# A decoder trunk on one core: scores of the undilated group with zero-padded queries, and the probabilities transposed one unit later

## Chip, core and metric

One core of a Trainium2 chip runs the whole kernel in one launch. The metric is the device time of one execution in microseconds. The kernel before took 806.12 us (median of 3 runs, 805.39 to 806.36).

## What is computed

Two layers on 256 tokens of width 1024, everything in float32. The first layer's mixer is dilated attention: three groups of 16 heads of 64, dilations 1, 4 and 16, each a causal band, whose outputs are mixed by a softmax over their log-denominators. The second layer's mixer is forgetting attention. After each mixer comes a SwiGLU block. The change is in the first group (dilation 1) of the first mixer:

```python
proj = (h @ w_in).reshape(B, S, N_GROUPS, 3, N_HEADS, HEAD_DIM)
for g, (window, dil) in enumerate(DILATED_PATTERNS):      # (128,1), (512,4), (2048,16)
    q = partial_rotary(proj[:, :, g, 0], pos)
    k = partial_rotary(proj[:, :, g, 1], pos)
    o, lse = dilated_band_attention(q, k, proj[:, :, g, 2], dil, window // dil)
...
s = einsum('bcnihd,bcnjhd->bcnhij', qb, kb) * D ** -0.5   # masked to the band
p = exp(s - m); den = p.sum(-1); o = (p / den) @ vb; lse = m + log(den)
```

## The kernel before

Precision is made by splitting: `split` turns a float32 value x into a high part (ScalarE copies it to the matmul type fp32r, L71) and a low part (VectorE takes x minus the high part, L72). `mm3` multiplies two split operands by three matmuls: high by high (L167), high by low (L168), low by high (L169). Every weight tile passes through this: SyncE loads `raw` (L86), ScalarE writes `wh`, VectorE writes `wl`. There are 5 `raw` buffers and 4 each of `wh` and `wl`.

The first mixer is a loop over 36 *units* (`a_units`), 9 for each *quad* of four heads (hq = 0 to 3): q and k of group 0, q and k of group 1, q and k of group 2, and the values of the three groups (quad 0 begins with the values of groups 1 and 2 and has the values of group 0 last). A unit is one projection: 48 matmuls of 256 columns into the PSUM tile `ps_mm`. Two heads share the 128 partitions, head h in rows 64h to 64h+63; two such pairs (`pr`) make a quad. After a q or k unit, `rotated` applies the rotary embedding: VectorE shuffles (L345) and multiplies by the cosine (L346), the sine is multiplied on VectorE for group 0 and on GpSimd for the others (L347), and VectorE adds (L348). For group 0 the result is split into one tile, `qkr`.

Work on the attention is put off by `later`, a table from unit to functions that are run after that unit's projection:

- `scores_a(quad, 0)` one unit after k of group 0: for each pair and each of two query blocks and two heads one `mm3`, 24 matmuls in all, into `ps_sc` (two buffers). A head's matmul contracts its 64 rows; k is the moving operand, read with every second element (`early`), since the tokens are kept in a permuted order. Then `softmax`: mask and scale (L238), maximum (L241) on VectorE, exponentials with sums on ScalarE (L232).
- `scores_a` for the groups 1 and 2 (L375, 16 matmuls of 64 columns for each group), and after group 2 `group_weights`, which scales the probabilities `p` (L248, four tiles on VectorE, two on GpSimd).
- `trans_a(quad, pr)` for each pair, after unit 9 hq + 10 + pr: three times four transposes (L254) into `ps_tr` (two buffers), each copied to `pt` by VectorE (L258). So the third group of four waits until the first copy has freed its buffer.
- `pv_a(quad, pr)`, after unit 9 hq + 11 + pr: probabilities by values (L265) into `ps_o`, whose result is split into `ot`.

The units 9 hq + 9 and following belong to the next quad, so the transposes of a quad stand among the projections of the next one; those of quad 3 run in `out_proj`. The framework's scheduler orders the instructions of each engine by priority; `first()` raises it. The tiles with tag `h` have four buffers: the two `xp` rows of the input at the start, `qkr`, and the rows `x` that the residual needs in `out_proj` (L495), loaded at units 24 and 28 (L452).

Of the kernel before, what the change touches and what calls it, by code (L numbers as in the profile page):

```python
# [10 lines left out]
F32 = mybir.dt.float32  # L11
F32R = mybir.dt.float32r
# [4 lines left out]
P = 128  # L17
D = 1024
S = 256
# [12 lines left out]
def trunk(ctx: ExitStack, tc: tile.TileContext, T, out):  # L32
    nc = tc.nc
# [3 lines left out]
    ap = ctx.enter_context(tc.tile_pool(name="ap", bufs=1))  # L37
    ps = ctx.enter_context(tc.tile_pool(name="ps", bufs=1, space=bass.MemoryType.PSUM))

    ALL = slice(None)  # L40

    def first():

        return tc.high_priority(offset=300)

    def psum(tag):
        return ps.tile([P, 512], F32, tag=tag, name=f"ps_{tag}", bufs=2)

    def hrow(name):
        return ap.tile([P, D], F32, tag="h", name=name, bufs=4)  # L50
# [7 lines left out]
    def const(name, shape):  # L58
        c = cst.tile(shape, F32, name=name)
        nc.sync.dma_start(c, T[name])  # L60
        return c
# [6 lines left out]
    def split(pair, view, src, early=True):  # L68
        hi, lo = pair
        with first() if early else nullcontext():  # L70
            nc.scalar.activation(view(hi), src, AF.Copy)  # L71
            nc.vector.tensor_tensor(view(lo), src, view(hi).bitcast(F32), op=ALU.subtract)  # L72
# [52 lines left out]
    def weights(nm, i):  # L125
        upto = order.index((nm, i)) + AHEAD
        while state["next"] <= min(upto, len(order) - 1):
            key = order[state["next"]]
            ready[key] = piece(key)
            state["next"] += 1  # L130
        return ready.pop((nm, i))
# [33 lines left out]
    def mm3(o, stat, mov, start, stop):  # L165
        (sh, sl), (mh, ml) = stat, mov
        nc.tensor.matmul(o, sh, mh, start=start, stop=False)  # L167
        nc.tensor.matmul(o, sh, ml, start=False, stop=False)  # L168
        return nc.tensor.matmul(o, sl, mh, start=False, stop=stop)  # L169

    def both(pair, *idx):
        return tuple(x[idx] for x in pair)


    def early(x, b):

        x = x.rearrange("p (n b) -> p b n", b=2)
        return x if b is None else x[:, b]
# [23 lines left out]
    def p_tile():  # L202
        return ap.tile([P, 512], F32, tag="p", name="p", bufs=8)
# [27 lines left out]
    def exps(s, nm, den, j):  # L231
        nc.scalar.activation(s, s, AF.Exp, bias=nm[:, j:j + 1], accum_out=den[:, j:j + 1])  # L232

    def softmax(sc, mask, nm, den, i, g):

        s = p_tile()
        f = lambda x: x.rearrange("p (a b) -> p a b", b=mask.shape[-1])
        nc.vector.scalar_tensor_tensor(f(s), f(sc), HD ** -0.5, mask, op0=ALU.mult, op1=ALU.add)  # L238
        m = nm.rearrange("p (i g) -> p i g", g=NG)[:, i, g]
        sv = s.rearrange("p (i g j) -> p i g j", i=m.shape[1], g=m.shape[2])  # L240
        nc.vector.tensor_reduce(m, sv, axis=AX.X, op=ALU.max, negate=True)  # L241
        for x in range(m.shape[1]):
            for y in range(m.shape[2]):
                exps(sv[:, x, y, :], nm, den, (i.start + x) * NG + g.start + y)
        return sv
# [21 lines left out]
    def stat_tile(tag, n):  # L267
        return ap.tile([P, n], F32, tag=tag, name=tag, bufs=3)
# [66 lines left out]
    x = []  # L335
# [3 lines left out]
    def rotated(o, tag, eng):  # L339

        q = ap.tile([P, 2, S], F32, tag=tag, name=tag, bufs=2)
        tmp = ap.tile([P, 2, S], F32, tag="qr", name="rt", bufs=3)
        ov = o.rearrange("p (a b) -> p a b", a=2)
        with first():
            nc.vector.stream_shuffle(tmp, ov, [i ^ 8 if i < ROT else i for i in range(32)])  # L345
            nc.vector.tensor_tensor(q, ov, rcos[:, None, :].to_broadcast([P, 2, S]), op=ALU.mult)  # L346
        eng.tensor_tensor(tmp, tmp, rsin[:, None, :].to_broadcast([P, 2, S]), op=ALU.mult)  # L347
        nc.vector.tensor_tensor(q, q, tmp, op=ALU.add)  # L348
        return q

    def scores_a(quad, g):

        q, k = quad["fm"][g, 0], quad["fm"][g, 1]
        nm, den, pt = quad["nm"], quad["den"], quad["pt"]
        hr = (slice(0, 64), slice(64, 128))
        if g == 0:
            for pr in range(2):
                sc = [psum("sc") for _ in range(2)]
                for qb in range(2):
                    for h in range(2):  # L360
                        mm3(sc[h][:, qb * S:(qb + 1) * S], both(q, hr[h], pr, slice(qb * P, (qb + 1) * P)),
                            [early(x[hr[h], pr, :], None) for x in k], True, True)
                for h in range(2):
                    pt[pr, h] = softmax(sc[h], mask0, nm, den, slice(h * 4 + pr * 2, h * 4 + pr * 2 + 2), slice(0, 1))
            return

        if g == 1:
            quad["sc"] = [psum("sc") for _ in range(2)]
        sc = quad["sc"]
        for b in range(4):  # L370
            for h in range(2):
                for a in range(2):
                    c = slice(b % 2 * P + a * 64, b % 2 * P + a * 64 + 64)
                    o = b * P + (g - 1) * 64
                    nc.tensor.matmul(sc[h][a * 64:a * 64 + 64, o:o + 64], q[hr[h], b // 2, c], k[hr[h], b // 2, c],  # L375
                                     start=True, stop=True)
        if g == 2:
            m = mask12[:, None, :].to_broadcast([P, 4, P])
            for h in range(2):
                pt[h] = softmax(sc[h], m, nm, den, slice(h * 4, h * 4 + 4), slice(1, NG))  # L380
# [54 lines left out]
    def later(i, fn, *a):  # L435
        due.setdefault(i, []).append((fn, a))

    quad = None
    for i, (hq, g, w) in enumerate(a_units):
        if i % 9 == 0:  # L440
            quad = {"hq": hq, "fm": {}, "pt": {}, "v": {}, "nm": stat_tile("nm", 24), "den": stat_tile("den", 24)}
        wt, o = lead[i] if i < 2 else (weights("a_in", hq * 9 + g * 3 + w), psum("mm"))
        if i == 1:
            rcos = const("rcos", [P, S])
            rsin = const("rsin", [P, S])
        if i == 2:
            mask0 = const("mask0", [P, 2, S])
            mask12 = const("mask12", [P, P])
        if i in (24, 28):
            x.append(hrow("x"))  # L450
            t = len(x) - 1
            nc.sync.dma_start(x[t], T["x"][t * P:(t + 1) * P, :])  # L452
        if w < 2:
            for c in range(2):
                proj_feat(xt, wt, o[:, c * S:(c + 1) * S], c)
            if i == 2:
                rb = psum("tr")
                for t in range(2):
                    nc.tensor.matmul(rb[:, t * P:(t + 1) * P], r_a[t].to_broadcast([P, P]), ident,
                                     start=True, stop=True)  # L460
                for c in (rcos, rsin):
                    nc.vector.tensor_tensor(c, c, rb[:, :S], op=ALU.mult)
                rt = ap.tile([P, 2], F32, tag="rt", name="rt", bufs=1)
                tmp = ap.tile([P, D], F32, tag="xn", name="rd", bufs=2)[:, :S].rearrange("p (b c) -> p b c", b=2)
                e = early(rb[:, :S], None)
                nc.vector.tensor_tensor(tmp, e, ident[:, None, :].to_broadcast([P, 2, P]), op=ALU.mult)
                nc.vector.tensor_reduce(rt, tmp, axis=AX.X, op=ALU.add)
            q = rotated(o, f"fm{w}", nc.vector if g == 0 else nc.gpsimd)
            if g == 0:
                y = ap.tile([P, 2, 2, S], F32R, tag="h", name="qkr", bufs=4)  # L470
                f, q = q, (y[:, 0], y[:, 1])
                split(q, lambda y: y, f)
            quad["fm"][g, w] = q
            if w == 1:
                later(i + 1, scores_a, quad, g)
                if g == 2:
                    later(i + 1, group_weights, quad)
                    for pr in range(2):
                        later(9 * hq + 10 + pr, trans_a, quad, pr)
                        later(9 * hq + 11 + pr, pv_a, quad, pr)  # L480
        else:
            for t in range(i < 2, 2):
                proj_tok(xt, wt, o[:, t * S:(t + 1) * S], t, g == 0)
            values_a(quad["v"], g, o)
        for fn, a in due.pop(i, ()):
            fn(*a)
# [253 lines left out]
    for i, (hq, w) in enumerate(b_units):  # L740
# [4 lines left out]
        if w < 2:  # L745
            for c in range(2):
                proj_feat(xt, wt, o[:, c * S:(c + 1) * S], c)
            q = ap.tile([P, 2, S], F32, tag=f"fm{w}", name=f"fm{w}", bufs=2)
# [8 lines left out]
        else:  # L757
            for t in range(2):
                proj_tok(xt, wt, o[:, t * S:(t + 1) * S], t)
            q = v_tile(o)  # L760
# [32 lines left out]
    r = rstd(parts)  # L793
# [73 lines left out]
```

## Time and profile before

| | us |
|---|---|
| median of 3 runs | 806.12 |
| the profiled execution | 805.15 |
| its span in the trace | 803.4 |
| TensorE busy | 787.4 |
| VectorE busy | 555.4 |
| ScalarE busy | 421.2 |
| GpSimd busy | 59.9 |

The profiled execution is 0.97 us below the median, and its time lies 1.75 us above the span. In the lists below a row has a start, a length, the engine (PE is TensorE, PEld its weight loads, DVE VectorE, ACT ScalarE, POOL GpSimd, SP SyncE), the line, the tiles out<-in, the form (for a matmul rows*columns of the weights, then partitions x elements) and the count; in brackets stands idle time of the engine ahead of it and what ended that. Matmuls overlap: a row's length runs to the modelled end of the result, so what a matmul costs the engine is read from the distance between starts. The dilated mixer's units run from about 10 to 264 us, its output projection to about 294 us.

### The profile page before, as it was taken

What the parts mean: (1) busy time and instruction counts of PE and PEld (TensorE: products, weight loads), DVE (VectorE), ACT (ScalarE), POOL (GpSimd) and SP (SyncE); (2) the same over time, 40 slices, a digit from 0 to 9 for tenths busy, and PEclk for the clock granted to TensorE, in tenths of its full rate; (3) what the DMA queues carried; (4) which work ended last, traced back from release to release, by engine and by line L of the source; (5) the groups of instructions that cost most, each with busy time, mean ns of one, the idle gap of its engine ahead of it and who ended that gap; (6) DMA issues with size and microseconds to landing.
All of it is one profiled execution on the core that took longest, in us unless ns stands there. A gap on an engine that the chain in (4) does not pass through costs nothing.

```text
span 803.4 us, 13954 instructions
## 1 busy us (share of the span) xinstructions
PE 787.4 (98%) x5564; PEld 702.4 (87%) x5564; DVE 555.4 (69%) x829; ACT 421.2 (52%) x819; POOL 59.9 (7%) x76
## 2 busy tenths in 40 slices
PE   8999999999999999999999999999999999999996
PEld 7989899899999789888888879988879888888885
DVE  6798997986986685555657555677766756556643
ACT  7756347447445365455556545364535655546532
POOL 0010111011010110000000001211111000000001
PEclk9999999999999999999999999999999999999999
DMA  8856253734634346655556434543316665655601
GB/s 293 271 158 217 79 184 109 251 106 141 211 130 159 105 162 211 208 180 189 179 205 230 165 133 146 184 171 130 95 40 236 212 207 171 198 179 205 218 1 52
DMA packets 38833, 135.00 MB, mean 168 GB/s; under 512 B 4592, under 2 KB 5360, under 8 KB 38768
## 3 DMA queue, kind: packets, MB, share of 16 engines
q1 hardware_dynamic: 38624, 133.85, 49.9%
q8 instruction: 43, 0.70, 0.3%
q10 hardware_dynamic: 144, 0.26, 0.1%
q14 instruction: 22, 0.18, 0.1%
HBM read 133.05 MB, written 1.05 MB: 167 GB/s over the span
## 4 chain that ended last, share of the span: by engine, by line
PE 82%; DVE 10%; ACT 3%; issue 3%; DMA 1%; SPq 0%; POOL 0%; POOLq 0%; DVEq 0%
PE ps_mm L167 10%; PE ps_mm L169 10%; PE ps_mm L168 10%; PE ps_tr L198 9%; PE ps_mm L198 9%; PE ps_tr L199 4%; PE ps_mm L199 4%; PE ps_sc L167 4%; PE ps_sc L168 4%; PE ps_sc L169 4%; DVE wl L72 4%; PE ps_o L167 3%; PE ps_o L168 3%; PE ps_o L169 3%; ACT wh L71 2%
## 5 line engine op out<-in xcount | busy, mean ns | idle before, releaser
L72 DVE TENSOR_TENSOR wl<-raw,wh 128x1024 fp32r<-128x1024 f32 (+1 forms) x242 | 299.7, 1256 | 133.9 <-ACT wh L71 133.7
L71 ACT ACTIVATE wh<-raw 128x1024 fp32r<-128x1024 f32 (+1 forms) x242 | 248.3, 1048 | 165.2 <-issue 51.6
L167 PE MATMUL ps_mm<-xt,wh 128*128 128x256 f32 x512 | 147.4, 288 | 0.0
L168 PE MATMUL ps_mm<-xt,wh 128*128 128x256 f32 x512 | 145.4, 284 | 0.0
L169 PE MATMUL ps_mm<-xt,wl 128*128 128x256 f32 x512 | 145.4, 284 | 0.0
L198 PE MATMUL ps_tr<-xt,wh 128*128 128x512 f32 x304 | 109.6, 400 | 0.0
L198 PE MATMUL ps_mm<-xt,wh 128*128 128x512 f32 x304 | 108.1, 396 | 0.0
L167 PEld LDWEIGHTS ps_mm<-xt,wh 128*128 128x128 f32 x512 | 97.9, 191 | 3.1 <-issue 2.3
L168 PEld LDWEIGHTS ps_mm<-xt,wh 128*128 128x128 f32 x512 | 98.0, 191 | 1.5 <-issue 1.5
L169 PEld LDWEIGHTS ps_mm<-xt,wl 128*128 128x128 f32 x512 | 97.9, 191 | 1.0 <-issue 1.0
L167 PE MATMUL ps_mm<-wh,xt 128*128 128x256 f32 x304 | 86.6, 285 | 0.8 <-ACT wh L71 0.8
L168 PE MATMUL ps_mm<-wl,xt 128*128 128x256 f32 x304 | 86.0, 284 | 0.3 <-DVE wl L72 0.3
L169 PE MATMUL ps_mm<-wh,xt 128*128 128x256 f32 x304 | 85.8, 283 | 0.0
L199 PE MATMUL ps_tr<-xt,wl 128*128 128x256 f32 x304 | 85.1, 280 | 0.0
L199 PE MATMUL ps_mm<-xt,wl 128*128 128x256 f32 x304 | 84.9, 279 | 0.0
L198 PEld LDWEIGHTS ps_tr<-xt,wh 128*128 128x128 f32 x304 | 57.1, 188 | 15.1 <-DVE low L557 1.5
L198 PEld LDWEIGHTS ps_mm<-xt,wh 128*128 128x128 f32 x304 | 57.1, 188 | 13.2
L232 ACT ACTIVATE p<-p,nm 128x64 f32<-128x64 f32 (+2 forms) x128 | 51.4, 407 | 29.3 <-DVE nm L241 17.9
L167 PEld LDWEIGHTS ps_mm<-wh,xt 128*128 128x128 f32 x304 | 58.5, 192 | 1.7 <-ACT wh L71 1.4
L168 PEld LDWEIGHTS ps_mm<-wl,xt 128*128 128x128 f32 x304 | 58.4, 192 | 0.7 <-DVE wl L72 0.5
L169 PEld LDWEIGHTS ps_mm<-wh,xt 128*128 128x128 f32 x304 | 58.4, 192 | 0.0
L199 PEld LDWEIGHTS ps_mm<-xt,wl 128*128 128x128 f32 x304 | 57.2, 188 | 0.5
(213 smaller groups left out, 1271.5 us busy)
## 6 DMA issues: line engine op xcount, KB each, us to landing
raw<-in_gu SPq DMA_DIRECT2D x88, 512.0 KB, 4.3
raw<-in_a_in SPq DMA_DIRECT2D x70, 512.0 KB, 4.6
raw<-in_dn SPq DMA_DIRECT2D x44, 512.0 KB, 4.0
raw<-in_b_in SPq DMA_DIRECT2D x24, 512.0 KB, 4.6
raw<-in_a_out SPq DMA_DIRECT2D x8, 512.0 KB, 3.6
raw<-in_b_out SPq DMA_DIRECT2D x8, 512.0 KB, 3.5
grow<-in_norms SPq DMA_DIRECT2D x4, 512.0 KB, 5.6
xp<-in_x_perm SPq DMA_DIRECT2D x4, 256.0 KB, 4.6
```

What stands on the lines that cost most here:

```text
L71: nc.scalar.activation(view(hi), src, AF.Copy)
L72: nc.vector.tensor_tensor(view(lo), src, view(hi).bitcast(F32), op=ALU.subtract)
L167: nc.tensor.matmul(o, sh, mh, start=start, stop=False)
L168: nc.tensor.matmul(o, sh, ml, start=False, stop=False)
L169: return nc.tensor.matmul(o, sl, mh, start=False, stop=stop)
L198: nc.tensor.matmul(o.rearrange("p (x s) -> p x s", x=2), wh, xt.full[:, k], start=k == 0, stop=False)
L199: nc.tensor.matmul(o[:, :S], wl, xt[0][:, k], start=False, stop=k == KT - 1)
L232: nc.scalar.activation(s, s, AF.Exp, bias=nm[:, j:j + 1], accum_out=den[:, j:j + 1])
```

## The change

It has two parts, and a row of the input is loaded later.

1. Group 0's q is split into two tiles `qzh` and `qzl` of 2 x 2 x 256 elements a partition: plane h holds head h's rows, and zeros in the other head's 64 rows. GpSimd writes the zeros (four memsets of 64 x 512 a quad, L472), ScalarE and VectorE split each half by itself (two instructions of 64 x 512 each instead of one of 128 x 512). k is split into `kr` with its tokens already reordered, so that a read of 256 columns is contiguous. A score matmul now contracts all 128 rows, the other head's being multiplied by zero, and each head has its own `ps_sc` tile right before its softmax. There are still 24 matmuls a quad. Three buffers of tag `h` are taken in each quad instead of two.
2. `trans_a` and `pv_a` are put off to the units 9 hq + 11 + pr and 9 hq + 12 + pr.
3. The second row `x` is loaded at unit 31 instead of 28.

```diff
         if g == 0:
             for pr in range(2):
-                sc = [psum("sc") for _ in range(2)]
-                for qb in range(2):
-                    for h in range(2):
-                        mm3(sc[h][:, qb * S:(qb + 1) * S], both(q, hr[h], pr, slice(qb * P, (qb + 1) * P)),
-                            [early(x[hr[h], pr, :], None) for x in k], True, True)
                 for h in range(2):
-                    pt[pr, h] = softmax(sc[h], mask0, nm, den, slice(h * 4 + pr * 2, h * 4 + pr * 2 + 2), slice(0, 1))
+                    sc = psum("sc")
+                    for qb in range(2):
+                        mm3(sc[:, qb * S:(qb + 1) * S], both(q, ALL, h, pr, slice(qb * P, (qb + 1) * P)),
+                            both(k, ALL, pr, ALL), True, True)
+                    pt[pr, h] = softmax(sc, mask0, nm, den, slice(h * 4 + pr * 2, h * 4 + pr * 2 + 2), slice(0, 1))
             return
...
-        if i in (24, 28):
+        if i in (24, 31):
...
+            if g == 0 and w == 0:
+                qz = tuple(ap.tile([P, 2, 2, S], F32R, tag="h", name=f"qz{y}", bufs=4) for y in "hl")
+                for y in qz:
+                    for h in range(2):
+                        nc.gpsimd.memset(y[64 - h * 64:128 - h * 64, h].bitcast(F32), 0.0)
             q = rotated(o, f"fm{w}", nc.vector if g == 0 else nc.gpsimd)
-            if g == 0:
-                y = ap.tile([P, 2, 2, S], F32R, tag="h", name="qkr", bufs=4)
+            if g == 0 and w == 0:
+                for h in range(2):
+                    r = slice(h * 64, h * 64 + 64)
+                    split(qz, lambda y: y[r, h], q[r])
+                q = qz
+            elif g == 0:
+                y = ap.tile([P, 2, 2, S], F32R, tag="h", name="kr", bufs=4)
                 f, q = q, (y[:, 0], y[:, 1])
-                split(q, lambda y: y, f)
+                split(q, lambda y: y.rearrange("p a (b n) -> p a b n", b=2), f.rearrange("p a (n b) -> p a b n", b=2))
...
-                        later(9 * hq + 10 + pr, trans_a, quad, pr)
-                        later(9 * hq + 11 + pr, pv_a, quad, pr)
+                        later(9 * hq + 11 + pr, trans_a, quad, pr)
+                        later(9 * hq + 12 + pr, pv_a, quad, pr)
```

What this does to the order is shown at three places; the tiles have their numbers, so that buffers can be told apart. First TensorE at the first score matmuls of quad 2. Before, they follow the transposes of the second pair of quad 1 (`p_1210` and `p_1215`), and the two heads' tiles `ps_sc` take turns:

```order
L254 MATMUL ps_tr_1933<-ident_78,p_1210 128x128 x2
L254 MATMUL ps_tr_1933<-ident_78,p_1215 128x128 x2
L254 MATMUL ps_tr_1940<-ident_78,p_1210 128x128 x2
L254 MATMUL ps_tr_1940<-ident_78,p_1215 128x128 x2
L167 MATMUL ps_sc_1954<-qkr_1829,qkr_1761 128x256
L168 MATMUL ps_sc_1954<-qkr_1829,qkr_1761 128x256
L169 MATMUL ps_sc_1954<-qkr_1829,qkr_1761 128x256
L167 MATMUL ps_sc_1955<-qkr_1829,qkr_1761 128x256
L168 MATMUL ps_sc_1955<-qkr_1829,qkr_1761 128x256
L169 MATMUL ps_sc_1955<-qkr_1829,qkr_1761 128x256
```

Now the same place, where the transposes ahead are those of the first pair (the row shown is the last of four, `p_1169`), and one head's tile is filled after the other:

```order
L254 MATMUL ps_tr_1925<-ident_78,p_1169 128x128 x2
L167 MATMUL ps_sc_1939<-kr_1850,qzh_1769 128x256
L168 MATMUL ps_sc_1939<-kr_1850,qzh_1769 128x256
L169 MATMUL ps_sc_1939<-kr_1850,qzl_1770 128x256
L167 MATMUL ps_sc_1939<-kr_1850,qzh_1769 128x256
L168 MATMUL ps_sc_1939<-kr_1850,qzh_1769 128x256
L169 MATMUL ps_sc_1939<-kr_1850,qzl_1770 128x256
L167 MATMUL ps_sc_1951<-kr_1850,qzh_1769 128x256
L168 MATMUL ps_sc_1951<-kr_1850,qzh_1769 128x256
L169 MATMUL ps_sc_1951<-kr_1850,qzl_1770 128x256
L167 MATMUL ps_sc_1951<-kr_1850,qzh_1769 128x256
L168 MATMUL ps_sc_1951<-kr_1850,qzh_1769 128x256
```

The four transposes of the pair's third group come next, and then the twelfth score matmul. So 11 score matmuls stand between the eighth transpose of the pair and the ninth; before, 11 projection matmuls stood there, and the scores came a unit later. Second VectorE at the copies of these transposes. Before, they stand behind the shuffle and cosine of quad 2's k (`ps_mm_1774`), among the steps that lead to the split of k:

```order
L345 STREAM_SHUFFLE rt_1824<-ps_mm_1774 128x512
L346 TENSOR_TENSOR fm1_1823<-ps_mm_1774,rcos_287 128x512
L258 COPY pt_1837<-ps_tr_1832 128x512
L258 COPY pt_1844<-ps_tr_1839 128x512
L347 TENSOR_TENSOR rt_1824<-rt_1824,rsin_289 128x512
L258 COPY pt_1851<-ps_tr_1846 128x512
L348 TENSOR_TENSOR fm1_1823<-fm1_1823,rt_1824 128x512
L72 TENSOR_TENSOR wl_2003<-raw_2004,wh_2002 128x1024
L72 TENSOR_TENSOR qkr_1829<-fm1_1823,qkr_1829 128x512
```

Now they stand behind the split of k and the shuffle and cosine of the next unit (`ps_mm_1863`), ahead of the softmax of the scores:

```order
L72 TENSOR_TENSOR kr_1850<-fm1_1844,kr_1850 128x512
L345 STREAM_SHUFFLE rt_1913<-ps_mm_1863 128x512
L346 TENSOR_TENSOR fm0_1912<-ps_mm_1863,rcos_287 128x512
L258 COPY pt_1923<-ps_tr_1918 128x512
L258 COPY pt_1930<-ps_tr_1925 128x512
L348 TENSOR_TENSOR fm0_1912<-fm0_1912,rt_1913 128x512
L258 COPY pt_1937<-ps_tr_1932 128x512
L238 SCALAR_TENSOR_TENSOR p_1946<-ps_sc_1939,mask0_330 128x512
```

The copies keep their distance behind a shuffle and a cosine, but one unit later. Third GpSimd, whose rows now hold the memsets; this is the stretch of quad 1, with the zeros of quad 2's low part between two sine multiplications:

```order
L347 TENSOR_TENSOR rt_1124<-rt_1124,rsin_289 128x512
L472 MEMSET qzl_1770 64x512 x2
L347 TENSOR_TENSOR rt_1258<-rt_1258,rsin_289 128x512
L347 TENSOR_TENSOR rt_1359<-rt_1359,rsin_289 128x512
L347 TENSOR_TENSOR rt_1457<-rt_1457,rsin_289 128x512
```

Before, the sine multiplications stood there alone. In quad 0 the scores stay where they were among the projections, and the transposes of quad 3 in `out_proj` keep their place.

## The prediction, made before the changed kernel ran

> **What bounds the kernel now.** I read the page first, then TensorE's list of waits, then its order of time around the scores.
>
> ```profile
> PE 787.4 (98%) x5564; PEld 702.4 (87%) x5564; DVE 555.4 (69%) x829; ACT 421.2 (52%) x819; POOL 59.9 (7%) x76
> ```
>
> TensorE is busy for 98% of the span, so a microsecond that it gains is one of the kernel, if nothing else is late then. What it waits for, from 28 us to the end (who for whom, us in total, times, longest):
>
> ```profile
> PE ps_sc L694 <- DVE p L702: 2.0, 4, 0.7
> PE ps_tr L254 <- DVE pt L258: 1.6, 2, 0.8
> PE ps_tr L161 <- DVE xn L156: 0.7, 1, 0.7
> PE ps_tr L254 <- DVE p L248: 0.7, 1, 0.7
> PE ps_sc L167 <- ACT qkr L71: 0.4, 1, 0.4
> PE ps_sc L167 <- ACT ah L71: 0.3, 1, 0.3
> ```
>
> No row names a weight (`wh`, `wl`): weights come in time. Three rows belong to this change: transposes wait for the copy of the one before (1.6, in quads 2 and 3) or for the scaled probabilities (0.7, quad 1), scores for the split of k (0.4). Now TensorE at the scores of quad 0:
>
> ```profile
> 39.88 0.28 PE L168 MATMUL ps_mm<-xt,wh 128*128 128x256 f32 x1
> 40.00 0.28 PE L169 MATMUL ps_mm<-xt,wl 128*128 128x256 f32 x1
> 40.39 0.48 PE L167 MATMUL ps_sc<-qkr 64*128 64x256 f32 x2
> 40.79 0.39 PE L167 MATMUL ps_mm<-xt,wh 128*128 128x256 f32 x1
> ...
> 41.46 0.48 PE L168 MATMUL ps_sc<-qkr 64*128 64x256 f32 x2
> 41.76 0.41 PE L169 MATMUL ps_sc<-qkr 64*128 64x256 f32 x2
> 41.99 0.41 PE L167 MATMUL ps_sc<-qkr 64*128 64x256 f32 x2
> ...
> 42.78 0.39 PE L167 MATMUL ps_mm<-xt,wh 128*128 128x256 f32 x1
> ...
> 43.60 0.28 PE L167 MATMUL ps_mm<-xt,wh 128*128 128x256 f32 x1
> 43.81 0.47 PE L167 MATMUL ps_sc<-qkr 64*128 64x256 f32 x1
> 44.11 0.40 PE L168 MATMUL ps_sc<-qkr 64*128 64x256 f32 x1
> 44.33 0.40 PE L169 MATMUL ps_sc<-qkr 64*128 64x256 f32 x1
> ...
> 45.35 0.38 PE L168 MATMUL ps_mm<-xt,wh 128*128 128x256 f32 x1
> 45.57 0.28 PE L169 MATMUL ps_mm<-xt,wl 128*128 128x256 f32 x1
> ...
> 46.61 0.47 PE L167 MATMUL ps_sc<-qkr 64*128 64x256 f32 x1
> ...
> 48.16 0.39 PE L168 MATMUL ps_mm<-xt,wh 128*128 128x256 f32 x1
> ```
>
> Read the distances between starts. A projection matmul over 128 rows costs 0.12 (39.88 to 40.00). A score matmul over 64 rows costs 0.22 alone (44.11 to 44.33). Two heads do run side by side (x2), but the pair takes 0.23 (41.76 to 41.99), 0.115 each: no more than makes up for the slower stream. Where no partner stands next to it, and in the second half of quad 0 none does, the matmul costs double.
>
> The Trainium skill, "TensorE: Matmul & The Clock Gate", section "Why this matters for your kernels", says that matmuls with few contraction rows should be sliced onto distinct row groups, which then run concurrently. That speaks against filling up with zeros: with 128-row speed in each half a pair would cost 0.12, the 96 score matmuls 5.8 us, and the change would add 5.8. The trace agrees that pairs start together, and not that this is a gain: 0.23 a pair. As the price before is measured, the rule gives no other time for the change.
>
> **The change, part by part.** All terms are against the profiled execution, 805.15 us (span 803.4), which is 0.97 below the median of 806.12.
>
> *Score matmuls.* In quad 0 the four batches take 40.39 to 40.79, 41.46 to 42.78, 43.81 to 45.35 and 46.61 to 48.16, together 4.81. Quad 2, in the same view:
>
> ```profile
> 157.32 0.48 PE L167 MATMUL ps_sc<-qkr 64*128 64x256 f32 x2
> ...
> 158.88 0.39 PE L167 MATMUL ps_mm<-xt,wh 128*128 128x256 f32 x1
> ...
> 159.22 0.29 PE L169 MATMUL ps_mm<-xt,wl 128*128 128x256 f32 x1
> 159.59 0.66 PE L254 MATMUL ps_tr<-ident,p 128*128 128x128 f32 x4
> ...
> 162.20 0.47 PE L167 MATMUL ps_sc<-qkr 64*128 64x256 f32 x1
> ...
> 164.29 0.38 PE L169 MATMUL ps_mm<-xt,wl 128*128 128x256 f32 x1
> ```
>
> Here 1.56 + 2.09 = 3.65, which I take for quads 1 to 3. The sum is 4.81 + 3 x 3.65 = 15.8. After, 96 matmuls have the form of the projections, 128 rows and 256 contiguous columns, at 0.12: 11.5. **Gain 4.3.** Why 64 rows are slow, the halved height or the reading of every second element, doesn't matter, since both go.
>
> *Changes of height.* The last projection matmul ahead of a batch takes 0.21 (43.60 to 43.81), the first one behind it 0.22 (45.35 to 45.57): 0.19 over the usual for a batch. There are 4 batches in quad 0 and, taken as in quad 2, 2 in each other, 10 in all. **Gain 1.9.**
>
> *Waits that go.* 1.6 at the copies in quads 2 and 3, 0.7 at the scaled probabilities and 0.4 at the split in quad 1; at 40.00 TensorE lost 0.39 - 0.12 - 0.09 = 0.18; at 159.22 it lost 0.37 - 0.12 = 0.25, and so in quad 3. Together 3.4. In the order of TensorE's instructions 114 projection matmuls stood between the scores of quad 0's last group and its first transposes, and now 144: 30 x 0.12 = 3.6 us more, which covers the 0.7 of the probabilities. In quads 2 and 3 the time between the eighth and the ninth transpose is 11 matmuls (1.3) as before, but the split of k, which shared VectorE with the copies, is done a unit earlier now; I take the 0.8 there as gone.
>
> *Waits that come.* VectorE and ScalarE split q in two halves each:
>
> ```profile
> 29.60:40.30 10.70, 10.68 (x90) 10.48 (x88) 10.70 (x18) 6.33 (x7) 0.00 (x0) 1.00 0.82 275
> 39.70 0.63 ACT L71 ACTIVATE qkr<-fm 128x512 fp32r<-128x512 f32 x1
> L72 DVE TENSOR_TENSOR qkr<-fm,qkr 128x512 fp32r<-128x512 f32 x8 | 5.4, 679 | 0.0
> L229 ACT ACTIVATE v<-ps_mm,rs 64x256 f32<-64x256 f32 x32 | 13.4, 464 | 2.5 <-PE ps_mm L169 1.8 <-POOL rs L141 0.6
> L214 ACT ACTIVATE v<-ps_mm,rt 128x256 f32<-128x256 f32 x8 | 3.4, 470 | 15.3 <-PE ps_mm L169 15.3
> ```
>
> Half the partitions take as long as all (464 ns against 470), so splitting q in halves costs one more instruction, 0.63 on ScalarE and 0.68 on VectorE, say 0.6 where they overlap. In the stretch ahead of quad 0's scores (first row: the length, then busy time of TensorE, weight loads, VectorE, ScalarE, GpSimd) VectorE is busy for all of 10.70 us. So its steps for k move by 0.6, with them ScalarE's split of k (from 39.70 to 40.33), which the scores at 40.39 wait for, and the wait there becomes 0.8. In quad 1 VectorE must scale, split k and copy in one stretch, and score matmuls that read the low part of k come 10 or so matmuls behind the transposes; between nothing and twice the 0.6 I take 0.6. In quads 2 and 3 the ninth transpose of the second pair waits for a copy that stands behind a shuffle, a cosine, one `wl` and the split of `ot`; between nothing and the 0.8 that such a wait takes now I take 0.4 each. Together 2.2. **Net gain of waits 1.2.**
>
> *What is hidden.* The zeros:
>
> ```profile
> L347 POOL TENSOR_TENSOR rt<-rt,rsin 128x512 f32<-128x512 f32 x16 | 20.7, 1296 | 153.8 <-DVE rt L345 153.8
> ```
>
> No memset of this size is in the trace. Bounds are nothing and this 1.3 us for 512 columns, 5.2 a quad; I take the middle, 2.6. GpSimd idles 153.8 us ahead of these very rows, so the cover is wide. The zeros of the next quad wait for a buffer that this quad's scores free, and behind them on GpSimd's queue stands the sine product of the next unit, whose sum VectorE waits for (L348); that unit ends 48 x 0.12 = 5.8 us after the scores begin. If the cover were gone, the sine product and with it VectorE's queue would come up to 2.6 later in a quad, with the softmax and the copies behind it. The Trainium skill, "SBUF — State Buffer", section "Who interferes with whom", says that a VectorE instruction with two SBUF inputs contends with a GpSimd instruction that reads SBUF, and not with one that only writes; by it the memsets take nothing from VectorE. No run here shows it yet.
>
> The moved row of x, in the view of its tile:
>
> ```profile
> L452 SPq DMA_DIRECT2D x<-in_x x2: 425/572/720, 147.9 to 210.4; - x2
> L495 DVE TENSOR_TENSOR h_a_out<-ps_sc,x x2: 679/679/679, 294.5 to 295.1; 128x512 f32<-128x512 f32 x2
> ```
>
> It is issued at 210.4 and read at 294.5. Three units later it is still some 60 us early. On SyncE's queue it now waits for a buffer that quad 3's scores free, and behind it stand the loads of the last a_in tile and of a_out; after 28 us no weight is waited for, and these are needed tens of microseconds later. I take 0; if that cover were gone, up to a unit (5.8, 48 x 0.12).
>
> Sum: 4.3 + 1.9 + 1.2 = 7.4, so 797.7 in the profiled execution's terms and 806.12 - 7.4 = **798.7** as a median.
>
> **The rivals.**
>
> *VectorE keeps the pace between quads 0 and 1.*
>
> ```profile
> 48.30:85.00 36.70, 36.18 (x351) 35.58 (x351) 34.17 (x50) 20.26 (x55) 5.95 (x5) 1.00 0.61 199
> ```
>
> It is busy 34.17 of 36.70 there, and TensorE would arrive 2.1 us earlier (4.8 - 2.9 for the score matmuls, 0.8 for the changes of height, less 0.6), with 0.7 more to do for VectorE. For it: 2.5 us of idle time is all there is. Against it: the first transposes come 3.6 us later. If it holds, TensorE hands back quad 0's 2.1 and the wait for k in quad 1 doubles to 1.2: gain 4.7, 801.4.
>
> *The scores stay slow at full height.* This one ends slower. If what halves the speed lies in these operands and not in the 64 rows or the stride, 96 matmuls cost 0.225 each, 21.6 instead of 15.8, and no partner runs beside them: 5.8 lost, 1.9 and 1.2 gained, 2.7 slower, 808.8. It decides from 15.8 + 3.1 = 18.9 us for 96, 0.197 a matmul. For it: another 64-row matmul with 256 contiguous columns is long too,
>
> ```profile
> L698 PE MATMUL ps_sc<-ck,selr 64*128 64x256 f32 x16 | 5.5, 464 | 0.0
> ```
>
> 464 ns where the projections show 0.28; so the stride alone isn't the cause. Against it: that points to the height, which goes.
>
> *The change moves nothing.* The scores' time is real, but something behind them, a copy or a load, is late by as much as TensorE is early: 806.1. Against it: the list of waits has no load in it, and the SwiGLU stage follows with the same loops. The transposes' delay alone could do it only if a copy held TensorE for 7 us.
>
> **How the numbers follow.** Forecast 0.73, VectorE's pace 0.13, nothing moved 0.08, slow scores 0.06. A change within 0.2% (1.6 us) can't be told from none here. So faster 0.86, same 0.08, slower 0.06. If no new wait comes, the gain is 9.6 (796.5); with the second case 4.7 (801.4). The zeros out of cover add up to 2.6 on one quad's softmax, of which I count a third. The range takes in these ends: 796.0 to 802.3.
>
> **What would show it.** Score matmuls `ps_sc<-kr` 0.12 apart, with projection matmuls 0.12 on both sides of a batch; no idle time of 0.8 ahead of the ninth transpose in quads 2 and 3; the first scores later than 40.39 by about 0.6; memsets on GpSimd with VectorE's rows no longer beside them. Scores 0.2 or more apart would make the forecast wrong, and so would waits on `p`, `pt` or `kr` of over 6 us in total.

## The result, and the profile after

The changed kernel takes 803.55 us (median of 10 runs, 802.57 to 804.92), the kernel before 805.69 in its 10 runs. The ratio is 0.997 with a 95% interval from 0.9959 to 0.998: faster by 0.3%, some 2.4 us. The forecast was 7.4. The profiled execution took 803.71 (span 801.9). The row of busy time and the waits of TensorE from 28 to 280 us, in the columns used before:

```profile
PE 782.3 (98%) x5564; PEld 701.9 (88%) x5564; DVE 554.8 (69%) x833; ACT 423.1 (53%) x823; POOL 68.6 (9%) x92
```

```profile
PE ps_tr L254 <- DVE pt L258: 2.4, 5, 0.7
PE ps_sc L167 <- ACT kr L71: 2.1, 2, 1.1
PE ps_sc L168 <- DVE kr L72: 1.7, 3, 0.6
```

TensorE's busy time fell by 5.1, between the 4.3 forecast for the score matmuls and the 6.2 with the changes of height; its waits at the transposes and for k rose from 2.7 (1.6, 0.7, 0.4) to 6.2. TensorE at the scores of quad 2, in order of time:

```profile
152.23 0.35 PE L167 MATMUL ps_sc<-kr,qzh 128*128 128x256 f32 x1
153.10 0.39 PE L168 MATMUL ps_sc<-kr,qzh 128*128 128x256 f32 x1 [0.51 <-DVE kr L72]
153.32 0.28 PE L169 MATMUL ps_sc<-kr,qzl 128*128 128x256 f32 x1
153.44 0.28 PE L167 MATMUL ps_sc<-kr,qzh 128*128 128x256 f32 x1
...
154.28 0.28 PE L168 MATMUL ps_sc<-kr,qzh 128*128 128x256 f32 x1
155.02 0.63 PE L254 MATMUL ps_tr<-ident,p 128*128 128x128 f32 x4 [0.47 <-DVE pt L258]
...
157.40 0.28 PE L167 MATMUL ps_mm<-xt,wh 128*128 128x256 f32 x1
157.52 0.28 PE L167 MATMUL ps_sc<-kr,qzh 128*128 128x256 f32 x1
...
158.84 0.28 PE L169 MATMUL ps_sc<-kr,qzl 128*128 128x256 f32 x1
158.96 0.28 PE L168 MATMUL ps_mm<-xt,wh 128*128 128x256 f32 x1
```

The distances between starts are what was forecast: 0.12 between score matmuls (153.32 to 153.44), twelve of them in 1.44 (157.52 to 158.96), and 0.12 on both sides of the batch. But the second score matmul stands 0.87 behind the first, for the low part of k, and the ninth transpose 0.74 behind the score matmul ahead of it. VectorE's queue at the same place says why:

```profile
146.07 1.40 DVE L72 TENSOR_TENSOR qzl<-fm,qzh 64x512 fp32r<-64x512 f32 x2
...
152.36 0.68 DVE L72 TENSOR_TENSOR kr<-fm,kr 128x512 fp32r<-128x512 f32 x1
...
152.97 0.74 DVE L345 STREAM_SHUFFLE rt<-ps_mm 128x512 f32<-128x512 f32 x1
153.60 0.67 DVE L346 TENSOR_TENSOR fm<-ps_mm,rcos 128x512 f32<-128x512 f32 x1
154.19 1.28 DVE L258 COPY pt<-ps_tr 128x512 f32<-128x512 f32 x2
```

The two halves of q's low part take 1.40, and VectorE works from there to the copies without a gap. It starts k's low part, 0.68 long, at 152.36, when the second score matmul, 0.12 behind the first, would have been due at 152.35; and it starts the copies at 154.19.

### The profile page after: what moved, and what is told of

Its sections match the earlier page's. It is cut to its first block, busy times and chain, and to the rows that moved or that the text cites. A ratio compares the mean times of both kernels' runs of the same rounds, so it can differ in the third digit from the quotient of the medians.

```text
span 801.9 us, 13994 instructions
## 1 busy us (share of the span) xinstructions
PE 782.3 (98%) x5564; PEld 701.9 (88%) x5564; DVE 554.8 (69%) x833; ACT 423.1 (53%) x823; POOL 68.6 (9%) x92
## 4 chain that ended last, share of the span: by engine, by line
PE 78%; DVE 10%; ACT 5%; issue 4%; DMA 1%; SPq 0%; POOL 0%; POOLq 0%; DVEq 0%
PE ps_tr L198 9%; PE ps_mm L198 9%; PE ps_mm L167 8%; PE ps_mm L169 8%; PE ps_mm L168 8%; PE ps_tr L199 4%; PE ps_mm L199 4%; PE ps_sc L167 4%; PE ps_sc L169 4%; PE ps_sc L168 4%; DVE wl L72 3%; PE ps_o L167 3%; PE ps_o L168 3%; PE ps_o L169 3%; ACT wh L71 2%
## 5 line engine op out<-in xcount | busy, mean ns | idle before, releaser
L72 DVE TENSOR_TENSOR wl<-raw,wh 128x1024 fp32r<-128x1024 f32 (+1 forms) x242 | 296.0, 1242 | 134.9 <-ACT wh L71 134.8
L167 PE MATMUL ps_mm<-wh,xt 128*128 128x256 f32 x304 | 86.6, 285 | 0.6 <-ACT wh L71 0.6
```

## The experiments

Each was timed against runs of the kernel before on the same chip. "Against before" is the ratio's distance from 1, times 806; kernels are compared by it. "Waits" is the sum of TensorE's waits for `p`, `pt`, `kr` and `qkr` in its list, 2.7 in the kernel before.

| kernel | median, us | ratio to before (95%) | against before, us | waits, us |
|---|---|---|---|---|
| changed | 803.55 | 0.997 (0.9959 to 0.998) | -2.4 | 6.2 |
| e1 padded only | 804.86 | 0.9982 (0.9968 to 0.9996) | -1.5 | 7.1 |
| e2 late only | 807.58 | 1.0014 (0.9994 to 1.0034) | +1.1 | 2.9 |
| e3 low q on GpSimd | 804.55 | 0.998 (0.9966 to 0.9993) | -1.6 | 5.5 |
| e4 scores later | 804.08 | 0.9974 (0.996 to 0.9988) | -2.1 | 7.2 |
| e5 64 rows, k in order | 801.14 | 0.9946 (0.9933 to 0.9959) | -4.4 | 4.4 |
| e6 128 rows, strided k | 812.14 | 1.0088 (1.0072 to 1.0105) | +7.1 | 4.8 |
| e7 changed, half the scaling on ScalarE | 801.7 | 0.9954 (0.9941 to 0.9966) | -3.7 | 4.8 |
| e8 before, half the scaling on ScalarE | 804.21 | 0.9985 (0.9975 to 0.9995) | -1.2 | 0.7 |
| e9 = e5 and half the scaling | 800.23 | 0.9932 (0.9919 to 0.9945) | -5.5 | 2.9 |
| e10 = e5 and late | 800.94 | 0.9944 (0.9932 to 0.9957) | -4.5 | 4.0 |
| e11 = e5 and q in halves | 805.3 | 0.9995 (0.9983 to 1.0008) | -0.4 | 8.0 |
| e12 = e10 and q in halves | 807.04 | 1.0013 (1.0004 to 1.0021) | +1.0 | 6.9 |
| e13 = e10 and half the scaling | 799.06 | 0.9915 (0.9902 to 0.9928) | -6.9 | 2.7 |

**First question: is it the order or VectorE's length that brings the waits?** Four kernels were compared. The change without the delay:

```diff
-                        later(9 * hq + 11 + pr, trans_a, quad, pr)
-                        later(9 * hq + 12 + pr, pv_a, quad, pr)
+                        later(9 * hq + 10 + pr, trans_a, quad, pr)
+                        later(9 * hq + 11 + pr, pv_a, quad, pr)
```

> The padded queries alone, with the transposes of the probabilities at their old place. The trace of the changed kernel shows score matmuls at 0.12 us as forecast, and about 8.4 us of waits of TensorE where 3.4 stood before. Theory A (order): the delay of the transposes puts the scores of quads 1 to 3 right behind the unit whose VectorE steps they need, so the waits for kr there (1.2 + 0.8 in quad 1, 0.5 each in quads 2 and 3) and most of those for pt (2.4 us in total) go when the order goes back, and the 0.7 us wait for the scaled probabilities in quad 1 comes back: 803.5 - 3.0 - 1.5 + 0.7 = 799.7. Theory B (length): the split of q in halves makes VectorE's queue late, wherever the transposes stand: 802.5 to 803.5. Theory C (GpSimd's work beside VectorE's makes it late): like B.

Measured: 804.86. Of the waits for k nearly all went in quads 1 to 3, and others came in their place:

```profile
PE ps_tr L254 <- DVE pt L258: 4.1, 4, 1.6
PE ps_tr L254 <- DVE p L248: 1.7, 2, 1.0
PE ps_sc L167 <- ACT kr L71: 1.0, 1, 1.0
PE ps_sc L168 <- DVE kr L72: 0.3, 1, 0.3
```

7.1 in all where the changed kernel has 6.2. Theory A, the order, falls: it wanted 799.7. (The 8.4 and 3.4 of the expectation count more than the waits of the table, which are 6.2 and 2.7.) The delay alone is the same two lines added to the kernel before:

> The kernel before with the transposes one unit later and nothing else changed. Theory A (order): scores come right behind their unit, so waits like those for kr and pt in quads 1 to 3 of the changed kernel come, some 2 to 3 us, less the 0.7 for the scaled probabilities: 807 to 808. Theory B (length of the split of q): without the split in halves no new wait, 805.0 to 805.7. Theory C: as B.

Measured: 807.58, which theory A forecast, but the waits are 2.9 against 2.7, so A's reason isn't there. The interval holds 1, and the median of the mean granted clocks is 0.996 where the kernel before has 0.998: 0.002 of 800 is 1.6 us, more than the 1.1. Then the low half of q was moved off VectorE:

```diff
-                    split(qz, lambda y: y[r, h], q[r])
+                    with first():
+                        nc.scalar.activation(qz[0][r, h], q[r], AF.Copy)
+                        nc.gpsimd.tensor_tensor(qz[1][r, h], q[r], qz[0][r, h].bitcast(F32), op=ALU.subtract)
```

> The changed kernel, with the low part of q made on GpSimd in place of VectorE, which takes 2 instructions of 0.7 us a quad off VectorE. Theory B (length): the scores' waits for kr (1.2 in quad 0, 2.0 in quad 1, 0.5 each in quads 2 and 3) shrink by up to 1.4 a quad, 3 us in all: 800.5. Theory A (order): waits shrink only in part, since the scores still stand right behind their unit: 801.5 to 802.5. Theory C (GpSimd's work beside VectorE's): no gain, 803.5 to 805, with VectorE's rows beside the new GpSimd rows longer.

Measured: 804.55, no gain, the time that theory C (GpSimd's work beside VectorE's) gave. The wait for ScalarE's part of k rose in quad 1 to 1.9. There an instruction of VectorE stands beside a new one of GpSimd; its group in this kernel from 81 to 83 us, and the same instruction (four times) in the kernel before:

```profile
L399 DVE TENSOR_TENSOR c<-e,z 128x24 f32<-128x24 f32 x1 | 1.3, 1277 | 0.0
```

```profile
L399 DVE TENSOR_TENSOR c<-e,z 128x24 f32<-128x24 f32 x4 | 0.7, 182 | 0.1
```

1277 ns where it took 182, so part of the relief was given back there. In quads 2 and 3 the waits fell, from 1.6 and 1.7 in the changed kernel to 1.0 each. And the median of the mean granted clocks is 0.995 here, 0.998 in the changed kernel: 0.003 of 800 is 2.4 us, enough to hide what the edit gained. So this run doesn't weigh the halves. Last, the scores a unit later:

```diff
-                later(i + 1, scores_a, quad, g)
+                later(i + (2 if g == 0 else 1), scores_a, quad, g)
```

> The changed kernel, with the undilated group's scores one unit of the projections later, so that they come behind the transposes and the product with v of the quad before, as they did before the change. Theory A (order): the waits for kr go in all quads (1.2 + 2.0 + 0.5 + 0.5 = 4.2), and part of those for pt: 799.3 or less. Theory B (length): the unit of time covers the 1.4 us too, in all quads: also 799.3; it differs from A in the kernel with the old transposes. Theory C: the same, if nothing else is late. If the softmax that is now a unit later is waited for, a new wait for p or for the buffers of the scores shows, and the time stays at 802 to 804.

Measured: 804.08. The waits for k are gone, and the same time is waited for elsewhere:

```profile
PE ps_tr L254 <- DVE pt L258: 5.7, 5, 1.9
PE ps_sc L167 <- DVE p L238: 1.5, 1, 1.5
```

Three orders with q in halves thus wait 6.2 to 7.2. What is constant isn't the place, so the next runs changed what the engines do.

**Second question: what made the scores slow, and is the padding needed for it?** The kernel before, with k split in order of its tokens and nothing else changed:

```diff
-                            [early(x[hr[h], pr, :], None) for x in k], True, True)
+                            both(k, hr[h], pr, ALL), True, True)
...
-                split(q, lambda y: y, f)
+                if w == 1:
+                    split(q, lambda y: y.rearrange("p a (b n) -> p a b n", b=2), f.rearrange("p a (n b) -> p a b n", b=2))
+                else:
+                    split(q, lambda y: y, f)
```

> The kernel before, with the split of k written in order of the keys, so that score matmuls over 64 rows read contiguous columns. If the 64 rows make them slow: still 0.22 us alone and 0.23 a pair, 3.6 to 4.8 us a quad, 805.5 to 806.5. If the reading of every second element does: 0.12 alone, 2.9 us or less a quad, and a time of 802 to 804.

Measured: 801.14, nearly twice the gain of the whole change. TensorE at quad 2 in this kernel, over 64 rows:

```profile
156.33 0.39 PE L167 MATMUL ps_sc<-qkr 64*128 64x256 f32 x2
156.55 0.29 PE L168 MATMUL ps_sc<-qkr 64*128 64x256 f32 x2
156.67 0.29 PE L169 MATMUL ps_sc<-qkr 64*128 64x256 f32 x2
156.79 0.28 PE L167 MATMUL ps_sc<-qkr 64*128 64x256 f32 x2
...
157.24 0.39 PE L167 MATMUL ps_mm<-xt,wh 128*128 128x256 f32 x1
...
161.43 0.28 PE L168 MATMUL ps_sc<-qkr 64*128 64x256 f32 x1
161.55 0.28 PE L169 MATMUL ps_sc<-qkr 64*128 64x256 f32 x1
```

A 64-row matmul takes 0.12 alone (161.43 to 161.55), and a pair of two heads takes 0.12 as well (156.55 to 156.67). The other side, the changed kernel with k read at every second element again:

```diff
-                            both(k, ALL, pr, ALL), True, True)
+                            [early(x[:, pr, :], None) for x in k], True, True)
...
-                split(q, lambda y: y.rearrange("p a (b n) -> p a b n", b=2), f.rearrange("p a (n b) -> p a b n", b=2))
+                split(q, lambda y: y, f)
```

> The changed kernel, with the score matmuls over 128 rows reading every second column of k. If the 64 rows were what made them slow: 0.12 us as before this edit, 2.9 a quad, 803 to 804. If the stride was: 0.22 each, 5.3 a quad, 9.5 us more of TensorE, of which part goes into its waits: 808 to 813.

Measured: 812.14, and in its timeline full rows at the old pace:

```profile
157.36 0.41 PE L169 MATMUL ps_sc<-kr,qzl 128*128 128x256 f32 x1
157.59 0.41 PE L167 MATMUL ps_sc<-kr,qzh 128*128 128x256 f32 x1
```

0.23 a matmul over 128 rows. So the stride halves the pace, at either height, and the height does nothing.

**Third question: what does VectorE's length cost?** In the changed kernel two of the four scalings of a quad were moved to ScalarE:

```diff
-                scale_p(pt[pr, h], cv[:, h, pr * 2:pr * 2 + 2, :1], nc.vector)
+                if h == 0:
+                    scale_p(pt[pr, h], cv[:, h, pr * 2:pr * 2 + 2, :1], nc.vector)
+                else:
+                    for qb in range(2):
+                        y = pt[pr, h][:, qb, 0]
+                        nc.scalar.activation(y, y, AF.Copy, scale=cv[:, h, pr * 2 + qb, :1])
```

> The changed kernel, with two of the four 128x512 scalings of the probabilities a quad made on ScalarE in four instructions in place of VectorE, which is busy without a gap from them to the scores of the next quad and takes 4.2 us there for four. Theory D (the stretch on VectorE is the limit, whatever stands in which order on TensorE): VectorE comes 2.1 us earlier in quads 1 to 3, and TensorE's waits for kr and pt there (2.4 in quad 1, 1.6 in quad 2, 1.3 in quad 3) go for the most part: 3 to 4 us less, 799.5 to 800.5. Theory A (order): the same waits shrink, since VectorE is earlier. Theory B (the split of q in halves): less, 1 us at most, since it stands behind. If ScalarE becomes late with the high parts of the weights instead, VectorE idles ahead of wl and nothing is won: 803 to 804.

Measured: 801.7, 1.3 us better by the ratios than the changed kernel, where theory D (VectorE's stretch is the limit in any order) wanted 3 to 4. The direction is D's, the size between D and B. The same edit in the kernel before:

> The kernel before, with the same two scalings on ScalarE. Theory D: TensorE waited there for p, pt and qkr for 2.7 us in all, so no more than that can go: 803.5 to 805. The difference to the changed kernel with the same edit is then 4 us or more, where the kernels without it differ by 2.1. If VectorE is not the limit of the changed kernel, that difference stays at about 2.

Measured: 804.21, 1.2 us gained and the waits down to 0.7. D wanted a distance of 4 or more between the two kernels with this edit; it is 2.5. So D as it was put falls too: the stretch is a limit of both kernels, not what sets them apart. Then the halves by themselves, in the kernel e5, with no zeros and no other order:

```diff
-                    split(q, lambda y: y, f)
+                    for h in range(2):
+                        r = slice(h * 64, h * 64 + 64)
+                        split(q, lambda y: y[r], f[r])
```

> The kernel before with k split in order of the keys, and q split in two halves of 64 partitions as the changed kernel does, but with no zeros and no other order: one more instruction a quad on ScalarE and one on VectorE. If the split in halves is what makes VectorE late: 1.4 us in place of 0.7 on VectorE four times, and TensorE waits that much longer in each quad: 803 to 804. If it is hidden: 801.1 to 801.7.

Measured: 805.3, above the range for the halves: 4.0 us more than e5 by the ratios, for eight instructions in all. VectorE from the shuffle of q to the copies of quad 3's stretch, first without the halves (e5), then with them (e11):

```profile
205.19 0.74 DVE L345 STREAM_SHUFFLE rt<-ps_mm 128x512 f32<-128x512 f32 x1
...
209.90 0.68 DVE L72 TENSOR_TENSOR qkr<-fm,qkr 128x512 fp32r<-128x512 f32 x1
...
210.51 0.74 DVE L345 STREAM_SHUFFLE rt<-ps_mm 128x512 f32<-128x512 f32 x1
211.15 0.67 DVE L346 TENSOR_TENSOR fm<-ps_mm,rcos 128x512 f32<-128x512 f32 x1
211.74 1.27 DVE L258 COPY pt<-ps_tr 128x512 f32<-128x512 f32 x2
```

```profile
207.88 0.74 DVE L345 STREAM_SHUFFLE rt<-ps_mm 128x512 f32<-128x512 f32 x1
...
212.59 1.40 DVE L72 TENSOR_TENSOR qkr<-fm,qkr 64x512 fp32r<-64x512 f32 x2
...
214.02 0.75 DVE L345 STREAM_SHUFFLE rt<-ps_mm 128x512 f32<-128x512 f32 x1
214.79 0.69 DVE L346 TENSOR_TENSOR fm<-ps_mm,rcos 128x512 f32<-128x512 f32 x1
215.40 1.28 DVE L258 COPY pt<-ps_tr 128x512 f32<-128x512 f32 x2
```

From the shuffle to the copies it is 6.55 without and 7.52 with the halves: 0.97 for one instruction more. The next shuffle started 0.61 after the one split, and starts 1.43 after the two. The list of waits passes it on: 8.0 against 4.4, 3.6 more in four quads. In quad 1 another cost comes with it. GpSimd's own scalings of `p` now start 0.38 ahead of VectorE's (85.53 and 85.91) instead of 1.10 (82.86 and 83.96 in e5), and beside them VectorE's first three take 3.59 instead of 2.71. The changed kernel, e1, e11 and e12, all with the halves, show this; the kernel before, e2, e5 and e10, without them, don't. Theory B, the halves, holds here. The delay beside e5 (the diff of e2):

> The kernel before with k split in order of the keys, and the transposes one unit later: the changed kernel without its zero rows. What it loses against the run without the delay (801.1) is the price of the delay, what the changed kernel (803.55) loses against it is the price of the zeros, the halves of the split and the lost pairs. If the order is the cause of the new waits: 802.5 to 803.5. If the split in halves is: 801.1 to 801.7.

Measured: 800.94, so the delay costs nothing when q is split in one piece. And the halves on top of that:

> The changed kernel without its zeros and with 64-row score matmuls: k in order of the keys, the transposes one unit later, q split in two halves of 64 partitions. At the old place of the transposes the halves cost 4.2 us (805.3 against 801.1). If the halves are the whole price of the padding, this kernel takes the time of the changed one, 803 to 804, and 2 to 3 us more than without them (800.9). If the zeros on GpSimd and the lost pairs are the price, it stays at 801 to 801.5.

Measured: 807.04, above everything expected. The waits rose by 2.9, to 6.9, which is the halves' price again; the rest shows in the clock. The windows of this kernel (start:end, length, busy times and counts of TensorE, weight loads, VectorE, ScalarE, GpSimd, then the granted clock):

```profile
86.00:91.50 5.50, 3.96 (x34) 3.34 (x34) 5.50 (x9) 2.68 (x3) 1.21 (x2) 1.00 0.12 28
91.50:95.50 4.00, 4.00 (x25) 3.68 (x22) 3.92 (x8) 0.00 (x0) 0.67 (x1) 0.57 0.25 93
...
156.50:160.50 4.00, 4.00 (x18) 3.74 (x19) 3.37 (x6) 1.13 (x5) 0.00 (x0) 0.57 0.18 66
```

Twice the clock falls to about half for some 3.5 us, each time behind the waits at the scores, and costs about 1.7 (4.0 us at 0.57). The mean granted clock of this kernel's twelve runs is 0.991 to 0.996, of the changed kernel's ten 0.997 to 0.999: near 0.004 of 800, 3.2 us. 2.9 and 3.2 make 6.1, where the ratios give 5.6.

**A faster version.** e5 with half the scaling on ScalarE (the diffs of e5 and e7), and the same with the delay:

> The kernel before with two edits: k split in order of the keys (801.1 alone), and two of the four scalings of the probabilities on ScalarE, as in the runs with that edit (1.3 us from the kernel before, 1.9 from the changed one). TensorE's waits in the run with k in order were 3.1 for pt and 0.7 for p. If VectorE's stretch ahead of the transposes is what they come from, most of the 3.8 goes: 798 to 799. If they come from the order, they stay: 800.5 to 801.1.

> k in order of the keys, the transposes one unit later, and two of the four scalings of the probabilities on ScalarE. TensorE's waits without the last edit were 2.7 for pt and 1.3 for qkr; at the old place of the transposes the last edit gave 0.9 (801.1 to 800.2). If it is VectorE's stretch behind the scalings that sets these waits, it gives 1.5 to 2.5 here, since the later transposes leave the scalings out of the path: 798.5 to 799.5. If order alone does: 800.5 to 801.

Measured: 800.23, between the two ranges given for it (pt still 2.2 and p 0.7), and 799.06, in the range for VectorE's stretch. The second is the fastest kernel of all, 0.85% below the kernel before, without a zero and with 64-row matmuls. Its waits:

```profile
PE ps_tr L254 <- DVE pt L258: 1.8, 4, 0.6
PE ps_sc L168 <- DVE qkr L72: 0.6, 1, 0.6
PE ps_mm L167 <- ACT v L229: 0.3, 1, 0.3
PE ps_sc L167 <- ACT qkr L71: 0.3, 1, 0.3
```

## Why the prediction was wrong

The step that failed is the waits: the forecast had 3.4 of them go and 2.2 come, and TensorE's list rose by 3.5. The changed kernel can be put together from the runs, in us by the ratios: k in order -4.4 (e5), the delay -0.1 (e10), the halves +5.5 (e12), and the zeros with full rows -3.4 (from e12 to the changed kernel; the order of the two heads and the later load of x come with this step and were not tried apart). The steps depend on their order; at the old place of the transposes the halves cost 4.0 (e5 to e11) and the zeros give 1.1 (e11 to e1). In both orders the halves are the loss, and the zeros none. That the halves cost the same in the changed kernel itself is concluded from these sums; no run has its zeros with q in one piece. The wait lists add up likewise: the faster scores alone bring 1.7 (2.7 to 4.4, e5), the delay takes 0.4 back (e10), the halves bring 2.9 (e12), and the last step takes 0.7. Why the zeros gain more in the later order is not shown; the clock's 3.2 is about their size, since e12 falls to half clock and the changed kernel doesn't.

- *Score matmuls*, gain 4.3: right. 24 take 2.88 a quad, 0.12 each. "Why 64 rows are slow ... doesn't matter, since both go" was true of this sum, and hid that one of the two was enough: e5 has the gain without the zeros.
- *Changes of height*, gain 1.9: right, 0.12 on both sides (157.40 to 157.52, 158.84 to 158.96). Without zeros it stays: e5's first matmul behind a batch stands 0.22 from the last, and pairs make up for it: its first twelve take 0.91 (156.33 to 157.24), the changed kernel's 1.44.
- *Waits that go*, 3.4: the 0.7 for `p` went. The 1.6 at the copies didn't. A sentence that failed is "the split of k ... is done a unit earlier now; I take the 0.8 there as gone": that split now stands right ahead of the copies (152.36, copies at 154.19), because scores and transposes came to the same place, both directly behind the unit whose steps VectorE was still making. The delay alone took only 0.4 off this wait (1.2 in e2).
- *Waits that come*, 2.2: this is the term that made the forecast wrong. The wait list has 6.2, of the very kinds named, and the text itself gave 6 as the mark. By quad the forecast was 0.8, 0.6, 0.4 and 0.4; the list has 1.1, 1.9, 1.6 and 1.7. I priced the added instruction at 0.6, and at 0.4 where the copies stand further behind it. It cost 0.97 in the queue (e11), up to the copies, since VectorE has no gap between q and them. In quad 0 the first score starts at 42.11 instead of 40.39; 0.61 of that is there already at the shuffle of q (30.00 instead of 29.39), and 1.11 is added behind it, where the forecast had 0.6. ScalarE's part of k, which that score waits for, itself stood idle 0.74 for VectorE's sum (L348). In quad 1 VectorE's four scalings take 4.19 instead of 3.38, beside GpSimd's, as in e11.
- *The sum*: 7.4 less the 4.0 missing in the waits is 3.4. A wait also costs more than its row: the one of 0.51 made the distance 0.87 instead of 0.12, 0.24 above the row, and the one of 0.47 made it 0.74, 0.15 above. An estimate from these two: some 10 waits instead of 4, at 0.2 each, take 1.2 more and leave 2.2, beside the measured 2.4.
- *What is hidden*: the zeros were. Four memsets a quad, 0.52 each, 2.1 where 2.6 was taken, on GpSimd, and no wait of TensorE names them:

```profile
L472 POOL MEMSET qzl<- 64x512 f32 x6 | 3.1, 521 | 7.8 <-PE ps_sc L169 7.5
```

- The rival *VectorE keeps the pace between quads 0 and 1* was nearest, with 801.4. It placed the loss in quads 0 and 1; the waits above the forecast are nearly all in quads 1 to 3, of which only the first was in its stretch. *The scores stay slow at full height* was out, but its evidence was misread: the 464 ns of the other 64-row matmul (L698) is a length, and its rows stand singly between other forms, so that no distance tells their pace. "So the stride alone isn't the cause" was wrong: e5 and e6 show that it is.
- The rule of "TensorE: Matmul & The Clock Gate" in the Trainium skill, section "Why this matters for your kernels", was put aside since pairs took 0.23. With k in order they take 0.12 (e5): the rule holds here, and the stride had hidden it. The 5.8 that the prediction worked out by it is 48 pairs at 0.12; where matmuls don't pair up, as for part of the second half of e5's quad 2 (161.43 to 161.55), it is 0.12 each.

## What to carry to other kernels

When a change removes two suspects at once, try each of them alone: the cheap one, writing k in reading order, had nearly twice the gain of the whole change. An instruction added to an engine that runs without a gap up to the next hand-over can cost its full length there or more (0.97 for one of 0.7 here), every time round, however low that engine's busy share is (69% here). Read a matmul's pace from the distances between starts, and judge what pairing two heads gains only when nothing else slows them.

## What the runs showed of the hardware

- Reading every second fp32 element as the moving operand costs 0.22 to 0.23 a matmul of 256 columns where contiguous reading costs 0.12, at 64 rows (before and e5) and at 128 (e6 and the changed kernel). The Trainium skill, "SBUF — State Buffer", section "Door 1: The DMA port swizzle", says that a line of 16 bytes is read at full bandwidth from two hits a line on. Every second fp32 is two hits a line, and the pace halved; the measurement decides.
- TensorE's clock fell to half for about 3.5 us (7 in e2) behind stretches with two waits close together: behind 0.93 and 0.61, 3.96 busy of 5.5 (e12), and behind 0.30 and 0.72, 2.98 busy of 4.0 (e2). It didn't behind 1.02 and 0.63 at the same place of the changed kernel, 4.35 busy of 6.0 (86 to 92 us). "TensorE: Matmul & The Clock Gate" in the Trainium skill, section "Why this matters for your kernels", names idle gaps of about 3 us as the limit; shorter ones were enough in e12 and e2. What decides between the two cases was not settled.
- VectorE and GpSimd hold each other up when both read, and a memset doesn't hold VectorE up. VectorE's scalings in the changed kernel's quad 1, first beside GpSimd's own scalings (84.4 to 86.6 us), then beside its memsets (87.23 to 87.7):

```profile
L248 DVE TENSOR_TENSOR p<-p,c 128x512 f32<-128x512 f32 x2 | 3.0, 1532 | 0.0
```

```profile
L248 DVE TENSOR_TENSOR p<-p,c 128x512 f32<-128x512 f32 x1 | 0.7, 679 | 0.0
```

1532 ns against 679 for the same instruction. GpSimd's two scalings take 2.82 there, and 2.05 in the kernel before, where VectorE's start 1.10 behind them instead of 0.37. That agrees with the rule that the prediction drew from the Trainium skill, "SBUF — State Buffer", section "Who interferes with whom".
